# Sums of weights and low parts of weights by accumulating DMAs in the seven-product feed-forwards of a two-layer decoder

## The chip, the cores and the metric

One core of a Trainium2 chip. Its engines are TensorE (PE, matrix products), VectorE (DVE), ScalarE (ACT), GpSimd (POOL) and SyncE (SP, which here issues DMAs), beside 16 DMA engines that move data between HBM and SBUF and within SBUF. The metric is the device time of one execution in microseconds, lower is better; outputs are fp32.

## The reference

A decoder trunk of two layers on x of 512 tokens by 1024 channels; each layer is a half-step feed-forward, a mixer of three parallel groups, a cross-attention, and a second half-step feed-forward, with an RMSNorm ahead of each and one at the end. The change touches the feed-forwards:

```python
def swiglu_ffn(h, w_gate, w_up, w_down):
    return (jax.nn.silu(h @ w_gate) * (h @ w_up)) @ w_down
...
        h = rmsnorm(x, ffn1_norm[l])
        x = x + 0.5 * swiglu_ffn(h, ffn1_w_gate[l], ffn1_w_up[l], ffn1_w_down[l])
...
        h = rmsnorm(x, ffn2_norm[l])
        x = x + 0.5 * swiglu_ffn(h, ffn2_w_gate[l], ffn2_w_up[l], ffn2_w_down[l])
```

D_MODEL is 1024, D_FF is 2816.

## The kernel before

The phases run in the order ffn1, mixer, attention, ffn2 for layer 0, then the same for layer 1, then the final norm. An instruction's tile names carry phase and layer: ffn20 is ffn2 of layer 0, ffn11 is ffn1 of layer 1.

Every fp32 product is three products of a faster type: each operand is split into a hi part, rounded by a copy on ACT, and a lo part, what remains, by a subtraction on DVE. `mm3` issues hi weight by hi activation (L307), hi by lo (L308) and lo by hi (L309) or, where weights are the moving side, the same three.

The first feed-forward, ffn1 of layer 0, is a plain one (`ffn`). The other three go through `ffn7`, which works out gate and up products by a seven-product scheme: tokens are cut in two halves, the contraction in two halves kh, and gate and up (z = 0 and 1) are the two column halves, so a unit's weights are four quarters (kh, z) = (0,0), (1,0), (0,1), (1,1). A unit is four column blocks of 128 out of 22, so there are six units in an `ffn7`, the last of two blocks. Each unit makes products 1, 2, 5, 6, 3, 7, 4 in that order, with weights and activations that are sums or differences of quarters; the down products of the unit before stand between them. The weights that a product reads are:

- products 1 and 2: (0,0) and (1,0) as loaded
- product 5: t1 = gate rows plus up rows of the upper half, four tiles of 128x512 (`mix1`, L475 to L478, on DVE)
- product 6: (0,0) after (0,1) += (1,1) and (0,0) += (0,1); product 7 reads that (0,1) (`mix2`, L484 to L486, by `sum_`, L480 to L482, on DVE, two additions of 128x1024 for a sum)
- product 4: (1,0) after (1,0) += (0,0) (`mix3`)

The sums are made in place, in the raw quarters. Three rules set the order. `steps` holds products and down products; weights are split two steps ahead of their product (`split2`: one row of 128x1024, L448 and L450, and two rows of 128x512, L458 and L459, for a quarter), raw loads and sums are put in `before` at given steps, and the Tile scheduler, which orders each engine's queue by a simulated timeline, moves single instructions from there. An engine works its queue in order: where an instruction waits, all behind it on that engine waits.

The first unit of each `ffn7` is special. Its norm is a `PairNorm`: while the phase before ends, its `take` loads the four quarters of unit 0 ("wr_first_ffn"), and POOL makes t1 (L221) and (0,1) += (1,1) (L223); unit 0's other two sums are `sum_` at the next steps. As the residual x of each of the four 128-token tiles is finished (`add_x`, L372), `half` makes the mean square on ACT (L188), adds the two columns up on DVE (L190), raises to the power -1/2 on POOL (L191), and `emit` scales the tile on DVE (L234) and forms the differences that products 5 and 6 need (L239, L246, L248, L250). `give` transposes each on PE (L256) and splits it into hi on ACT (L258) and lo on DVE (L259). The splits of unit 0's weights for products 5 and on are issued after the last of these for product 5 (`marks`). The names that the steps use: xp and xc are transposed activations, the number behind the phase being tile and product; wh and wl are a weight's hi and lo ("wl_ffn20_0p10": unit 0, product 1, first row); px, py and pz are the accumulators of the products.

```python
G.tensor_tensor(out=ss[:, 3:4], in0=ss[:, 2:3], in1=nhalf[:, 0:1], op=ALU.pow)
...
if 2 <= i + 2 < 7:
    for z in norm.marks:
        es.enter_context(tc.issue_after(z))
w[i + 2] = steps[i + 2][1]()
```

Of the kernel before, what the change touches and what calls it, by code (L numbers as in the profile page):

```python
# [17 lines left out]
P = 128  # L18
# [26 lines left out]
def trunk_kernel(ctx: ExitStack, tc: tile.TileContext, io, out, phases=None):  # L45
    nc = tc.nc
    V, A, G, T = nc.vector, nc.scalar, nc.gpsimd, nc.tensor
    ADD, SUB, MUL = ALU.add, ALU.subtract, ALU.mult
# [41 lines left out]
    def vt(name, shape=(P, 512), dt=F32):  # L90
        return vp.tile(list(shape), dt, tag="V", name=name)
# [4 lines left out]
    def st(name, shape=(P, 512), dt=F32):  # L96
        return ssp.tile(list(shape), dt, tag="S", name=name)
# [36 lines left out]
    def tsl(t):  # L134
        return slice(t * P, (t + 1) * P)
# [68 lines left out]
    HK = NK // 2  # L204
# [227 lines left out]
    def ffn7(which, l, norm, nxt):  # L432


        wg, wu, wd = (io[f"{which}_w_{n}"][l] for n in ("gate", "up", "down"))
        units = [(f, min(4, NF - f)) for f in range(0, NF, 4)]
        hts, kept = {}, []
        steps, before, later = [], {}, []
        at_step = {}

        def split2(raws, name):

            got = []
            for s, raw in enumerate(raws):
                whole = s == 0 and len(raws) == 2
                if whole:
                    h = wp.tile(list(raw.shape), F32R, tag="wh", name=f"wh_{name}{s}")
                    A.activation(out=h, in_=raw, func=AF.Copy)  # L448
                    lo = wp.tile(list(raw.shape), F32R, tag="wl", name=f"wl_{name}{s}")
                    V.tensor_tensor(out=lo, in0=raw, in1=h.bitcast(F32), op=SUB)  # L450
                    got += [(h[:, k, :], lo[:, k, :]) for k in range(2)]
                    continue
                for k, r in enumerate([raw] if len(raws) == 4 else [raw[:, k, :] for k in range(2)]):
                    if len(raws) == 4 and s < 2:
                        h, lo = (wp.tile(list(r.shape), F32R, tag=f"w{z}", name=f"w{z}_{name}{s}") for z in "hl")
                    else:
                        h, lo = (st(f"w{z}_{name}{s}{k}", tuple(r.shape), F32R) for z in "hl")
                    A.activation(out=h, in_=r, func=AF.Copy)  # L458
                    V.tensor_tensor(out=lo, in0=r, in1=h.bitcast(F32), op=SUB)  # L459
                    got.append((h, lo))  # L460
            return got

        class Unit:
# [10 lines left out]
            def mix1(self):  # L474
                a, b = self.raw[0, 0], self.raw[0, 1]  # L475
                t1 = self.raw["t1"] = [vt(f"wt_{self.nm}{k}", (P, self.W)) for k in range(HK)]
                for k in range(HK):
                    V.tensor_tensor(out=t1[k], in0=a[k // 2][:, k % 2, :], in1=b[k // 2][:, k % 2, :], op=ADD)  # L478

            def sum_(self, to, other):  # L480
                for a, b in zip(self.raw[to], self.raw[other]):
                    V.tensor_tensor(out=a, in0=b, in1=a, op=ADD)  # L482

            def mix2(self):  # L484
                self.sum_((0, 1), (1, 1))
# [77 lines left out]
        for u, un in enumerate(us):  # L563
            b = len(steps)
# [812 lines left out]
```

## Time and profile before

| | |
|---|---|
| median of 3 runs | 2134.53 us (2134.12 to 2137.26) |
| profiled execution | 2135.13 us |
| its span | 2133.0 us |
| mean granted clock of PE | 0.987 |
| PE busy | 2065.5 us (97%) |
| DVE busy | 1551.3 us (73%) |
| ACT busy | 917.0 us (43%) |
| POOL busy | 356.8 us (17%) |
| DMA | 229.92 MB, mean 108 GB/s |

The profiled execution is the one that the trace shows, and its durations add up to its own time. Span is first to last instruction; what lies between it and the execution's time is before and after. A busy share is an average over the span. PEclk, the granted clock, is 1.00 at full speed.

### The profile page before, as it was taken

The numbers are of one execution on the slowest core, as the hardware profiler recorded it, in microseconds if no ns is written. First come the engines' busy times: TensorE is split into PE (matmuls) and PEld (weight loads), VectorE is DVE, ScalarE is ACT, GpSimd is POOL, SyncE is SP. The second block draws the span as 40 slices with busy tenths as digits, with TensorE's granted clock in tenths as the row PEclk, the third lists the DMA queues.
The fourth block names the chain that finished last, engine by engine and source line by source line (L and its number), as shares of the span: only waits on it lengthen the run. The fifth ranks groups of instructions, "written<-read, shape, count | busy, mean of one in ns | idle before, by whom it ended". The sixth has DMA issues, their size and how long they took to land.

```text
span 2133.0 us, 27561 instructions
## 1 busy us (share of the span) xinstructions
PE 2065.5 (97%) x10228; PEld 1732.9 (81%) x10228; DVE 1551.3 (73%) x2574; ACT 917.0 (43%) x1528; POOL 356.8 (17%) x349
## 2 busy tenths in 40 slices
PE   7999999999999999999999999999999999999998
PEld 6778788888788878888878888888877887888886
DVE  5755677579855788787688877666996458887765
ACT  4423333334534464454445444444344345554443
POOL 0377000155400200000110000013661020000000
PEclk9999999998999999999999999999999999999999
DMA  5332445343421323332314223263443232332222
GB/s 170 101 104 82 117 150 165 108 137 107 125 88 60 119 80 119 119 119 79 119 40 147 83 88 108 80 217 97 122 134 109 70 134 79 119 107 91 74 60 84
DMA packets 226750, 229.92 MB, mean 108 GB/s; under 512 B 38478, under 2 KB 152888, under 8 KB 226616
## 3 DMA queue, kind: packets, MB, share of 16 engines
q1 hardware_dynamic: 225952, 227.10, 34.3%
q8 instruction: 80, 1.31, 0.3%
q10 hardware_dynamic: 664, 1.07, 0.1%
q14 instruction: 54, 0.44, 0.1%
HBM read 213.77 MB, written 12.58 MB: 106 GB/s over the span
## 4 chain that ended last, share of the span: by engine, by line
PE 83%; DVE 8%; DMA 3%; ACT 3%; issue 2%; POOL 1%; SPq 1%; DVEq 0%; POOLq 0%; ACTq 0%
PE pxffn L308 6%; PE pxffn L309 6%; PE pxffn L307 6%; PE pddffn L308 5%; PE pddffn L309 5%; PE pddffn L307 5%; PE pzffn L307 3%; PE pzffn L308 3%; PE pzffn L309 3%; PE pdffn L309 2%; PE pdffn L307 2%; PE pdffn L308 2%; DVE cacc L1053 1%; PE qps L308 1%; PE qps L309 1%
## 5 line engine op out<-in xcount | busy, mean ns | idle before, releaser
L308 PE MATMUL pddffn<-wl_dffn,hhffn 128*128 128x512 f32 x480 | 188.9, 394 | 0.0
L309 PE MATMUL pddffn<-wh_dffn,hlffn 128*128 128x512 f32 x480 | 188.1, 392 | 0.0
L307 PE MATMUL pddffn<-wh_dffn,hhffn 128*128 128x512 f32 x480 | 185.8, 391 | 0.0
L1053 DVE SCALAR_TENSOR_TENSOR cacc<-ch,convw,cacc 128x510 f32<-128x510 f32 (+28 forms) x174 | 127.8, 735 | 6.2 <-ACT cacc L1051 2.5
L374 DVE SCALAR_TENSOR_TENSOR x<-pddffn,x 128x512 f32<-128x512 f32 x120 | 82.2, 686 | 62.8 <-PE pddffn L309 62.8
L308 PEld LDWEIGHTS pddffn<-wl_dffn,hhffn 128*128 128x128 f32 x480 | 90.2, 188 | 18.2
L309 PEld LDWEIGHTS pddffn<-wh_dffn,hlffn 128*128 128x128 f32 x480 | 90.2, 188 | 18.0
L307 PEld LDWEIGHTS pddffn<-wh_dffn,hhffn 128*128 128x128 f32 x480 | 89.8, 188 | 18.3
L221 POOL TENSOR_TENSOR wt_first_ffn<-wr_first_ffn,wr_first_ffn 128x512 f32<-128x512 f32 x12 | 16.8, 1426 | 503.3 <-DMA wr_first_ffn<-in_ffn_w_up_dram 503.3
L482 DVE TENSOR_TENSOR wr_ffn<-wr_ffn,wr_ffn 128x1024 f32<-128x1024 f32 (+1 forms) x90 | 98.4, 1110 | 0.1
L300 POOL TENSOR_TENSOR wl_pl<-wr_pl,wh_pl 128x1024 fp32r<-128x1024 f32 x4 | 9.6, 2404 | 486.0 <-ACT wh_pl L298 486.0
L459 DVE TENSOR_TENSOR wl_dffn<-wr_dffn,wh_dffn 128x512 fp32r<-128x512 f32 x60 | 42.0, 705 | 39.7 <-PE pxffn L308 18.2
L535 ACT ACTIVATE hhffn<-htffn 128x512 fp32r<-128x512 f32 x60 | 35.6, 594 | 80.7 <-PE htffn L529 80.6
L307 PE MATMUL pgffn<-xh_ffn,wh_gffn 128*128 128x512 f32 x168 | 66.2, 394 | 0.0
L308 PE MATMUL pgffn<-xl_ffn,wh_gffn 128*128 128x512 f32 x168 | 66.0, 393 | 0.0
L309 PE MATMUL pgffn<-xh_ffn,wl_gffn 128*128 128x512 f32 x168 | 65.9, 392 | 0.0
L309 PE MATMUL puffn<-xh_ffn,wl_uffn 128*128 128x512 f32 x168 | 65.8, 392 | 0.0
L307 PE MATMUL puffn<-xh_ffn,wh_uffn 128*128 128x512 f32 x168 | 65.8, 392 | 0.0
L308 PE MATMUL puffn<-xl_ffn,wh_uffn 128*128 128x512 f32 x168 | 65.8, 392 | 0.0
L191 POOL TENSOR_TENSOR ss_final<-ss_final,nhalf 128x1 f32<-128x1 f32 x4 | 2.2, 550 | 350.2 <-DVE ss_final L190 350.2
L307 PE MATMUL pdffn<-wh_dffn,h_ffffn 128*128 128x512 f32 x144 | 57.9, 402 | 2.1 <-DVE sffn L394 2.1
L300 POOL TENSOR_TENSOR wl_v<-wr_v,wh_v 128x1024 fp32r<-128x1024 f32 x22 | 53.5, 2441 | 35.4 <-ACT wh_v L298 25.7
(745 smaller groups left out, 6735.7 us busy)
## 6 DMA issues: line engine op xcount, KB each, us to landing
wr_dffn<-in_ffn_w_down_dram SPq DMA_DIRECT2D x78, 512.0 KB
wr_ffn<-in_ffn_w_up_dram SPq DMA_DIRECT2D x48, 512.0 KB
wr_ffn<-in_ffn_w_gate_dram SPq DMA_DIRECT2D x48, 512.0 KB
wr_gffn<-in_ffn_w_gate_dram SPq DMA_DIRECT2D x21, 512.0 KB
wr_uffn<-in_ffn_w_up_dram SPq DMA_DIRECT2D x21, 512.0 KB
wr_k<-in_xattn_wk_dram SPq DMA_DIRECT2D x16, 512.0 KB
wr_v<-in_xattn_wv_dram SPq DMA_DIRECT2D x16, 512.0 KB
wr_q<-in_xattn_wq_dram SPq DMA_DIRECT2D x16, 512.0 KB
```

The costliest lines, as they stand in the source:

```text
L191: G.tensor_tensor(out=ss[:, 3:4], in0=ss[:, 2:3], in1=nhalf[:, 0:1], op=ALU.pow)
L221: G.tensor_tensor(out=t1[k], in0=a[k // 2][:, k % 2, :], in1=b[k // 2][:, k % 2, :], op=ADD)
L300: (eng or V).tensor_tensor(out=lo, in0=raw, in1=h.bitcast(F32), op=SUB)
L307: T.matmul(ps, lhsT=wh, rhs=ah, start=first, stop=False, skip_group_check=skip)
L308: T.matmul(ps, lhsT=wh, rhs=al, start=False, stop=False, skip_group_check=skip)
L309: T.matmul(ps, lhsT=wl, rhs=ah, start=False, stop=last, skip_group_check=skip)
L374: V.scalar_tensor_tensor(out=x_, in0=ps, scalar=scale, in1=x_, op0=MUL, op1=ADD)
L459: V.tensor_tensor(out=lo, in0=r, in1=h.bitcast(F32), op=SUB)
L482: V.tensor_tensor(out=a, in0=b, in1=a, op=ADD)
L535: A.activation(out=h, in_=pt, func=AF.Copy)
L1053: V.scalar_tensor_tensor(out=acc[:, d:], in0=h[:, 0:S - d], scalar=cw[:, TAPS - 1 - d:TAPS - d], in1=acc[:, d:], op0=MUL, op1=ADD)
```

## The change

Three kinds of DVE work in `ffn7` become DMAs. An accumulating DMA (`accum_op=ADD`) adds what it moves to what stands in its destination; POOL issues all of these.

1. `mix1`: t1 of units 1 to 5 is no longer added up from the raw quarters. SP loads the gate rows from HBM into t1, and POOL issues DMAs that add the up rows from HBM to it. That is 60 loads and 60 accumulating DMAs, of 256 KB each in full units and 128 KB in the last.
2. `sum_`: every sum of quarters is an accumulating DMA from SBUF to SBUF, 90 in all, of 512 KB each in full units, those of unit 0 among them.
3. `low`: in unit 0 the lo parts of products 1 and 2 are made by a negated copy on ACT (raw weight into lo) and an accumulating DMA that adds the raw weight to it. The negated copy rounds to the type of lo just as the hi copy does, so what remains in lo is the raw weight less its hi part. That is six copies and six DMAs (512 KB for a row of 128x1024, 256 KB for one of 128x512) in each of the three `ffn7`.

DVE's queue is 180 rows shorter (2501 to 2321), POOL's 180 longer (343 to 523), ACT's 18 longer (1416 to 1434), SP's 60 longer.

```diff
--- before.py
+++ after.py
@@ -434,11 +434,19 @@
 
         wg, wu, wd = (io[f"{which}_w_{n}"][l] for n in ("gate", "up", "down"))
         units = [(f, min(4, NF - f)) for f in range(0, NF, 4)]
+        by_dma = (1, 2)
         hts, kept = {}, []
         steps, before, later = [], {}, []
         at_step = {}
 
-        def split2(raws, name):
+        def low(lo, raw, h, adding):
+            if adding:
+                A.activation(out=lo, in_=raw, func=AF.Copy, scale=-1.0)
+                G.dma_start(out=lo, in_=raw, accum_op=ADD)
+            else:
+                V.tensor_tensor(out=lo, in0=raw, in1=h.bitcast(F32), op=SUB)
+
+        def split2(raws, name, adding=False):
 
             got = []
             for s, raw in enumerate(raws):
@@ -447,7 +455,7 @@
                     h = wp.tile(list(raw.shape), F32R, tag="wh", name=f"wh_{name}{s}")
                     A.activation(out=h, in_=raw, func=AF.Copy)
                     lo = wp.tile(list(raw.shape), F32R, tag="wl", name=f"wl_{name}{s}")
-                    V.tensor_tensor(out=lo, in0=raw, in1=h.bitcast(F32), op=SUB)
+                    low(lo, raw, h, adding)
                     got += [(h[:, k, :], lo[:, k, :]) for k in range(2)]
                     continue
                 for k, r in enumerate([raw] if len(raws) == 4 else [raw[:, k, :] for k in range(2)]):
@@ -456,7 +464,7 @@
                     else:
                         h, lo = (st(f"w{z}_{name}{s}{k}", tuple(r.shape), F32R) for z in "hl")
                     A.activation(out=h, in_=r, func=AF.Copy)
-                    V.tensor_tensor(out=lo, in0=r, in1=h.bitcast(F32), op=SUB)
+                    low(lo, r, h, adding)
                     got.append((h, lo))
             return got
 
@@ -475,11 +483,15 @@
                 a, b = self.raw[0, 0], self.raw[0, 1]
                 t1 = self.raw["t1"] = [vt(f"wt_{self.nm}{k}", (P, self.W)) for k in range(HK)]
                 for k in range(HK):
-                    V.tensor_tensor(out=t1[k], in0=a[k // 2][:, k % 2, :], in1=b[k // 2][:, k % 2, :], op=ADD)
+                    r0 = k * P
+                    nc.sync.dma_start(out=t1[k], in_=wg[r0:r0 + P, self.f0 * P:self.f0 * P + self.W])
+                for k in range(HK):
+                    r0 = k * P
+                    G.dma_start(out=t1[k], in_=wu[r0:r0 + P, self.f0 * P:self.f0 * P + self.W], accum_op=ADD)
 
             def sum_(self, to, other):
                 for a, b in zip(self.raw[to], self.raw[other]):
-                    V.tensor_tensor(out=a, in0=b, in1=a, op=ADD)
+                    G.dma_start(out=a, in_=b, accum_op=ADD)
 
             def mix2(self):
                 self.sum_((0, 1), (1, 1))
@@ -501,7 +513,7 @@
                                 k == HK - 1, True)
                     for t in range(2):
                         post(t)
-                steps.append((run, lambda: split2(self.raw[src], f"{self.nm}p{i}")))
+                steps.append((run, lambda: split2(self.raw[src], f"{self.nm}p{i}", self.u == 0 and i in by_dma)))
 
             def keep(self, c, name):
                 def post(t):
```

Line numbers below L437 move; `low` is L442 to L447 in the changed kernel, with the negated copy on L444 and its DMA on L445, the hi copy of a whole row on L456, t1's load and DMA on L487 and L490 and the sum's DMA on L494.

POOL's queue at the start of ffn2 of layer 0, before: (0,1) += (1,1) by two additions, then the powers of the four token tiles (ss_ffn20*t*).

```order
L221 TENSOR_TENSOR wt_first_ffn202_6379<-wr_first_ffn20001_6363,wr_first_ffn20011_6371 128x512
L221 TENSOR_TENSOR wt_first_ffn203_6380<-wr_first_ffn20001_6363,wr_first_ffn20011_6371 128x512
L223 TENSOR_TENSOR wr_first_ffn20010_6369<-wr_first_ffn20110_6373,wr_first_ffn20010_6369 128x1024
L223 TENSOR_TENSOR wr_first_ffn20011_6371<-wr_first_ffn20111_6375,wr_first_ffn20011_6371 128x1024
L191 TENSOR_TENSOR ss_ffn200_6404<-ss_ffn200_6404,nhalf_99 128x1
L191 TENSOR_TENSOR ss_ffn201_6443<-ss_ffn201_6443,nhalf_99 128x1
L191 TENSOR_TENSOR ss_ffn202_6501<-ss_ffn202_6501,nhalf_99 128x1
L191 TENSOR_TENSOR ss_ffn203_6554<-ss_ffn203_6554,nhalf_99 128x1
```

The same place in the changed kernel; wr_first_ffn20*kz s* is quarter (k,z), row s.

```order
L223 TENSOR_TENSOR wr_first_ffn20010_6369<-wr_first_ffn20110_6373,wr_first_ffn20010_6369 128x1024
L223 TENSOR_TENSOR wr_first_ffn20011_6371<-wr_first_ffn20111_6375,wr_first_ffn20011_6371 128x1024
L191 TENSOR_TENSOR ss_ffn200_6404<-ss_ffn200_6404,nhalf_99 128x1
L494 DMA wr_first_ffn20001_6363<-wr_first_ffn20011_6371 128x1024
L191 TENSOR_TENSOR ss_ffn201_6443<-ss_ffn201_6443,nhalf_99 128x1
L445 DMA wl_ffn20_0p211_6626<-wr_first_ffn20101_6367 128x512
L191 TENSOR_TENSOR ss_ffn202_6501<-ss_ffn202_6501,nhalf_99 128x1
L494 DMA wr_first_ffn20101_6367<-wr_first_ffn20001_6363 128x1024
L445 DMA wl_ffn20_0p10_6602<-wr_first_ffn20000_6361 128x1024
L445 DMA wl_ffn20_0p20_6617<-wr_first_ffn20100_6365 128x1024
L494 DMA wr_first_ffn20000_6361<-wr_first_ffn20010_6369 128x1024
L191 TENSOR_TENSOR ss_ffn203_6554<-ss_ffn203_6554,nhalf_99 128x1
```

The powers of the last three tiles now stand between DMAs; the low of product 1's first row (0p10) stands behind the sum into (1,0) row 1, and the last power behind the sum into (0,0) row 0, which overwrites what the DMA of 0p10 reads.

PE's queue where product 1 of unit 0 of the same phase begins, before: pxffn20_0*t* is its accumulator for token tile t of each half.

```order
L256 MATMUL xp_ffn2011_6478<-ident_90,xn_ffn2010_6476 128x128 x4
L307 MATMUL pxffn20_00_6640<-wh_ffn20_0p10_6600,xc_ffn201_6387 128x512
L256 MATMUL xp_ffn2012_6487<-ident_90,xn_ffn2011_6485 128x128 x4
L308 MATMUL pxffn20_00_6640<-wl_ffn20_0p10_6602,xc_ffn201_6387 128x512
L309 MATMUL pxffn20_00_6640<-wh_ffn20_0p10_6600,xc_ffn201_6387 128x512
L307 MATMUL pxffn20_00_6640<-wh_ffn20_0p10_6600,xc_ffn201_6387 128x512
L308 MATMUL pxffn20_00_6640<-wl_ffn20_0p10_6602,xc_ffn201_6387 128x512
L309 MATMUL pxffn20_00_6640<-wh_ffn20_0p10_6600,xc_ffn201_6387 128x512
```

And in the changed kernel:

```order
L256 MATMUL xp_ffn2011_6478<-ident_90,xn_ffn2010_6476 128x128 x4
L307 MATMUL pxffn20_00_6646<-wh_ffn20_0p10_6600,xc_ffn201_6387 128x512
L256 MATMUL xp_ffn2012_6487<-ident_90,xn_ffn2011_6485 128x128 x4
L307 MATMUL pxffn20_01_6647<-wh_ffn20_0p10_6600,xc_ffn201_6387 128x512
L307 MATMUL pyffn20_00_6706<-wh_ffn20_0p20_6615,xc_ffn202_6388 128x512
L308 MATMUL pxffn20_00_6646<-wl_ffn20_0p10_6602,xc_ffn201_6387 128x512
L309 MATMUL pxffn20_00_6646<-wh_ffn20_0p10_6600,xc_ffn201_6387 128x512
L308 MATMUL pxffn20_01_6647<-wl_ffn20_0p10_6602,xc_ffn201_6387 128x512
L307 MATMUL pxffn20_00_6646<-wh_ffn20_0p10_6600,xc_ffn201_6387 128x512
L308 MATMUL pxffn20_00_6646<-wl_ffn20_0p10_6602,xc_ffn201_6387 128x512
```

A first hi product for the second token tile and one of product 2 (pyffn20) moved ahead of the first product that reads the low wl_ffn20_0p10.

DVE's queue between the column sums (L190) of the third and the last token tile of that norm, before:

```order
L234 SCALAR_TENSOR_TENSOR xn_ffn2020_6534<-x2_103,ss_ffn202_6501,gb_ffn200_6357 128x512
L234 SCALAR_TENSOR_TENSOR xn_ffn2021_6536<-x2_103,ss_ffn202_6501,gb_ffn201_6358 128x512
L450 TENSOR_TENSOR wl_ffn20_0p10_6602<-wr_first_ffn20000_6361,wh_ffn20_0p10_6600 128x1024
L450 TENSOR_TENSOR wl_ffn20_0p20_6614<-wr_first_ffn20100_6365,wh_ffn20_0p20_6612 128x1024
L239 TENSOR_TENSOR xs_ffn202_6538<-xn_ffn2021_6536,xn_ffn2020_6534 128x512
L372 TENSOR_TENSOR x3_104<-pwo0_31_6557,x3_104 128x512
L482 TENSOR_TENSOR wr_first_ffn20000_6361<-wr_first_ffn20010_6369,wr_first_ffn20000_6361 128x1024
L259 TENSOR_TENSOR xc_ffn201_6387<-xp_ffn2011_6478,xc_ffn201_6387 128x4x128
L259 TENSOR_TENSOR xc_ffn202_6388<-xp_ffn2012_6487,xc_ffn202_6388 128x4x128
L250 TENSOR_TENSOR xn_ffn2020_6534<-xn_ffn2000_6418,xn_ffn2020_6534 128x512
L190 TENSOR_SCALAR ss_ffn203_6554<-ss_ffn203_6554 128x1
L482 TENSOR_TENSOR wr_first_ffn20100_6365<-wr_first_ffn20000_6361,wr_first_ffn20100_6365 128x1024
```

And in the changed kernel:

```order
L190 TENSOR_SCALAR ss_ffn202_6501<-ss_ffn202_6501 128x1
L259 TENSOR_TENSOR xc_ffn201_6387<-xp_ffn2001_6420,xc_ffn201_6387 128x4x128
L234 SCALAR_TENSOR_TENSOR xn_ffn2020_6534<-x2_103,ss_ffn202_6501,gb_ffn200_6357 128x512
L234 SCALAR_TENSOR_TENSOR xn_ffn2021_6536<-x2_103,ss_ffn202_6501,gb_ffn201_6358 128x512
L259 TENSOR_TENSOR xc_ffn202_6388<-xp_ffn2002_6429,xc_ffn202_6388 128x4x128
L239 TENSOR_TENSOR xs_ffn202_6538<-xn_ffn2021_6536,xn_ffn2020_6534 128x512
L250 TENSOR_TENSOR xn_ffn2020_6534<-xn_ffn2000_6418,xn_ffn2020_6534 128x512
L372 TENSOR_TENSOR x3_104<-pwo0_31_6557,x3_104 128x512
L259 TENSOR_TENSOR xc_ffn201_6387<-xp_ffn2011_6478,xc_ffn201_6387 128x4x128
L190 TENSOR_SCALAR ss_ffn203_6554<-ss_ffn203_6554 128x1
L259 TENSOR_TENSOR xc_ffn202_6388<-xp_ffn2012_6487,xc_ffn202_6388 128x4x128
L234 SCALAR_TENSOR_TENSOR xn_ffn2030_6587<-x3_104,ss_ffn203_6554,gb_ffn200_6357 128x512
```

The two lows of products 1 and 2 (L450) and the sums into (0,0) and (1,0) (L482) no longer stand on DVE between the tile's parts.

## Rows read from the trace of the kernel before

**Rows 1.** The page's busy times, share of the span and instructions of each engine.

```profile
PE 2065.5 (97%) x10228; PEld 1732.9 (81%) x10228; DVE 1551.3 (73%) x2574; ACT 917.0 (43%) x1528; POOL 356.8 (17%) x349
```

**Rows 2.** Busy times by stretch, in later units; the columns stand in the first line.

```profile
core 0: us, PE busy (x) PEld busy (x) DVE busy (x) ACT busy (x) POOL busy (x), PEclk, DMA share, GB/s
800.00:900.00 100.00, 100.00 (x455) 82.69 (x454) 81.40 (x111) 44.90 (x67) 0.00 (x0) 1.00 0.41 127
```

**Rows 3.** The same view at the first units of ffn20, ffn11 (two) and ffn21.

```profile
745.00:760.00 15.00, 12.06 (x55) 9.35 (x54) 14.32 (x24) 10.49 (x18) 0.00 (x0) 0.89 0.06 11
1100.00:1120.00 20.00, 16.77 (x76) 13.23 (x75) 17.38 (x27) 11.90 (x20) 0.00 (x0) 0.91 0.11 28
1120.00:1130.00 10.00, 9.17 (x40) 7.25 (x40) 6.15 (x8) 5.51 (x9) 0.00 (x0) 1.00 0.95 334
1775.00:1795.00 20.00, 16.88 (x77) 13.38 (x77) 18.62 (x29) 11.99 (x21) 1.25 (x1) 0.91 0.10 26
```

**Rows 4.** Timeline of PE: start, duration, line, tiles; in brackets idle before it, releaser.

```profile
736.67 0.49 PE L308 MATMUL pxffn<-wl_ffn_0p,xc_ffn 128*128 128x512 f32 x1
...
747.97 1.03 PE L256 MATMUL xp_ffn<-ident,xs_ffn 128*128 128x128 f32 x8
750.27 0.63 PE L256 MATMUL xp_ffn<-ident,xs_ffn 128*128 128x128 f32 x4 [1.27 <-DVE xc_ffn L259]
752.24 0.68 PE L307 MATMUL pxffn<-wh_ffn_0p,xc_ffn 128*128 128x512 f32 x1 [1.34 <-ACT xc_ffn L258]
```

**Rows 5.** Timeline of DVE in the same stretch.

```profile
734.62 2.35 DVE L450 TENSOR_TENSOR wl_ffn_0p<-wr_first_ffn,wh_ffn_0p 128x1024 fp32r<-128x1024 f32 x2
...
738.10 1.21 DVE L482 TENSOR_TENSOR wr_first_ffn<-wr_first_ffn,wr_first_ffn 128x1024 f32<-128x1024 f32 x1
...
741.03 0.20 DVE L190 TENSOR_SCALAR ss_ffn<-ss_ffn 128x1 f32<-128x1 f32 x1
...
742.81 1.41 DVE L234 SCALAR_TENSOR_TENSOR xn_ffn<-x,ss_ffn,gb_ffn 128x512 f32<-128x512 f32 x2 [0.45 <-POOL ss_ffn L191]
```

**Rows 6.** Timeline of POOL at the first units of ffn20 and ffn11.

```profile
741.31 1.46 POOL L191 TENSOR_TENSOR ss_ffn<-ss_ffn,nhalf 128x1 f32<-128x1 f32 x1 [8.49 <-DVE ss_ffn L190]
...
1063.32 2.40 POOL L223 TENSOR_TENSOR wr_first_ffn<-wr_first_ffn,wr_first_ffn 128x1024 f32<-128x1024 f32 x1 [0.74 <-DMA wr_first_ffn<-in_ffn_w_up_dram]
1071.18 5.58 POOL L223 TENSOR_TENSOR wr_first_ffn<-wr_first_ffn,wr_first_ffn 128x1024 f32<-128x1024 f32 x1 [5.46 <-DMA wr_first_ffn<-in_ffn_w_up_dram]
1088.53 0.55 POOL L191 TENSOR_TENSOR ss_ffn<-ss_ffn,nhalf 128x1 f32<-128x1 f32 x1 [11.77 <-DVE ss_ffn L190]
```

**Rows 7.** Groups by line on DVE, whole kernel: count, busy us, mean ns, idle before.

```profile
L482 DVE TENSOR_TENSOR wr_ffn<-wr_ffn,wr_ffn 128x1024 f32<-128x1024 f32 (+1 forms) x90 | 98.4, 1110 | 0.1
L478 DVE TENSOR_TENSOR wt_ffn<-wr_ffn,wr_ffn 128x512 f32<-128x512 f32 (+1 forms) x60 | 36.0, 634 | 9.4 <-DMA wr_ffn<-in_ffn_w_up_dram 9.3
```

**Rows 8.** Timelines of DVE, ACT and PE in unit 2 of ffn20.

```profile
845.84 1.22 DVE L482 TENSOR_TENSOR wr_ffn<-wr_ffn,wr_ffn 128x1024 f32<-128x1024 f32 x1
...
857.29 1.06 ACT L448 ACTIVATE wh_ffn_2p<-wr_ffn 128x1024 fp32r<-128x1024 f32 x1 [1.61 <-PE pyffn L309]
...
865.75 0.39 PE L307 MATMUL pxffn<-wh_ffn_2p,xc_ffn 128*128 128x512 f32 x1
```

**Rows 9.** Timeline of ACT at the first unit of ffn20.

```profile
728.83 0.63 ACT L458 ACTIVATE wh_ffn_0p<-wr_first_ffn 128x512 fp32r<-128x512 f32 x1 [5.06 <-PE pwo L309]
...
732.21 2.00 ACT L448 ACTIVATE wh_ffn_0p<-wr_first_ffn 128x1024 fp32r<-128x1024 f32 x2
```

**Rows 10.** Transfers in the chain of waits: start, duration, destination, source (512 KB; sdy 256 KB).

```profile
1530.06 3.40 DMA sdy<-ssw
1537.28 3.66 DMA wr_k<-in_xattn_wk_dram
...
1737.60 5.66 DMA wr_first_ffn<-in_ffn_w_gate_dram
```

**Rows 11.** Timelines of ACT and PE where unit 1 of ffn20 begins.

```profile
776.39 1.05 ACT L448 ACTIVATE wh_ffn_1p<-wr_ffn 128x1024 fp32r<-128x1024 f32 x1
...
781.17 0.62 PE L307 MATMUL pxffn<-wh_ffn_1p,xc_ffn 128*128 128x512 f32 x2
```

## The prediction

> **What bounds the kernel now.** I began with the busy times: TensorE (PE) is busy 97% of the span and VectorE (DVE) 73% [rows 1]. Such shares are averages, so next came the busy times by stretch: from 800 to 900 us, in the later units of a seven-product feed-forward, PE is busy in every microsecond at full clock, and DVE 81% [rows 2]. DVE time that is taken away there buys nothing. PE has something to give only where it idles, and I found one such stretch in each of the three seven-product feed-forwards, at the start of product 6 of the first unit [rows 3]. From 745 to 760 us PE is busy 12.06 of 15, so 2.94 us idle, at a mean granted clock of 0.89: on the busy part, 11% of 12.06 is 1.3 us. From 1100 to 1120 it is 3.23 us idle at 0.91, from 1775 to 1795 3.12 us at 0.91. All three together hold 9.3 us of idle time and about 4 us of clock: 13 us is all that there is to win.
>
> Last came what PE waits for at 750 us, followed back by the timelines. Product 6 starts at 752.24 after a hi-half copy of ACT, and the transposes ahead of it, 750.27, after DVE [rows 4]. DVE has run almost without a gap since 742.81, where it waited for POOL's power at 741.31 [rows 5, 6]. That power came late because DVE made the column sum for it (L190) only at 741.03, behind a sum of weights at 738.10 and two lows of weights, 2.35 us, at 734.62 [rows 5]. So DVE is the bound of this stretch, and what stands on it there is just what the change takes off.
>
> **The change part by part.**
>
> *t1 and the sums of the later units.* The change takes 90 sums, 98.4 us, and 60 t1 additions, 36.0 us, off DVE [rows 7]. In the later units PE covers all of it [rows 2]: no gain. Their price could only be lateness. In unit 2 the sums into (0,0) began at 845.84 and product 6, their first reader on PE, at 865.75; the last hi copy for it ran at 857.29 for 1.06 us [rows 8]. If copies and lows keep some 9 of these 20 us, a landing may take about 11 us before PE sees it. If that cover is gone, each of 15 later units pays the rest. I take nothing.
>
> *Lows of products 1 and 2.* For each of three first units six subtractions leave DVE: two of 128x1024 (2.35 us together [rows 5]) and four of 128x512, about 0.7 each, so 5.2 us, and four sums of 1.2 us. ACT takes on six negated copies, two of 1.00 and four of 0.63 by its own hi copies [rows 9]: 4.5 us. POOL issues ten accumulating DMAs.
>
> *What replaces them on the critical stretch.* No row shows an accumulating DMA, nor any that POOL issues. The nearest rows: 512 KB from HBM took 3.66 and 5.66 us, 256 KB from SBUF 3.40 [rows 10]. An accumulating DMA reads its destination too, so for 512 KB (t512) I take the slow end, 5.7, and for 256 KB (t256) 3.4, which can't well be below it by more. The ends I keep for t512 are 3.7, and twice the slowest, 11.3, every destination byte being moved twice. Anything below 3.7 gains nothing more, as there is no wait left to end.
>
> The Trainium skill's page "DMA: Bandwidth & Descriptors", section "Anatomy of one DMA — SWDGE (gpsimd) path", fits 2.0 us plus the bytes at 436 GB/s to a DMA that GpSimd issues: an estimate of 3.2 us for 512 KB, which no run here shows. By it the sum would be that of rival 1.
>
> The chain in ffn2_0: ACT's copy for product 2's last quarter row ran at 728.83 for 0.63 us [rows 9]; the negated copy stands beside it, so its DMA leaves POOL at about 730.1. POOL's next sum, into (1,0), overwrites what that DMA reads and waits for its landing, 733.5. Behind it stands the DMA of product 1's first low (wl 0p10), whose negated copy is done at about 733.3; it lands at 733.5 + 5.7 = 739.2. PE read that low at 736.67 [rows 4]; two hi matmuls of 0.22 us (455 in 100 us [rows 2]) now go first, so PE wants it at 737.1. Stall: 2.1 us. On the same queue the last power (L191) stands behind a sum that waits for the same landing: it runs at about 739.8, where it ended at 742.77 before (741.31 + 1.46 [rows 6]). DVE, relieved, is ready for it, so product 6's chain comes over 2 us earlier than 752.24. PE would be through product 2 and the transposes at 747.97 + 1.03 = 749.0 [rows 4], say 749.3 to its next matmul; with the stall product 6 starts at 751.4: 0.8 us earlier than before. Of the 1.3 us of clock none or all comes back, as PE still idles 2.1 us, only sooner: 0.8 to 2.1, middle 1.4. ffn2_1 has the same order and the same gap: again 1.4.
>
> *ffn1_1.* Here the lows of products 1 and 2 are made some 20 us before they are read, and all of POOL's DMAs for them stand ahead of its first power at 1088.53 [rows 6]. The last DVE rows before the gap are unchanged. I count nothing; the bounds are the 3.2 us idle there as a gain and rival 3 as a loss.
>
> Sum: 2 x 1.4 = 2.8 off 2135.13, the profiled execution, is 2132.3. That execution stands 0.6 above the median of 2134.53, so against the runs I forecast **2132** (2131.7 rounded). A measurement of this kernel can tell about 0.2%, 4.3 us, from no change: the forecast is no change that it can tell, with a small gain in it.
>
> **The rivals.** Product 6 starts at 749.3 + (730.1 + t256 + t512 - 737.1) = 742.3 + t256 + t512, as long as that is later than 749.3. The two DMA times decide, and 9.9 us together is where gain turns to loss.
>
> 1. *Quick DMAs.* With 3.4 and 3.7 product 6 starts at 749.4, 2.8 earlier, and 1.3 of clock comes back: 4.1 twice, 8.2, so 2126.9, and 2126.3 against the median. For it: the quickest row [rows 10], and DMA engines all but idle there, share 0.06 [rows 3]. Against: the second read, and that three DMAs stand one behind another.
>
> 2. *Slow accumulating DMAs*, the case on the other side: one queue, POOL's, holds both product 1's low and the last power, and from 9.9 us on for the pair the change loses. At 5 and 8 us product 6 starts at 755.3, 3.1 late, twice 6.2: 2141.3. At 6.8 and 11.3 it is 8.2 late, twice 16.4: 2151.5. For it: nothing in the trace bounds the read and write of a destination. Against: plain 512 KB stay under 6 us [rows 10].
>
> 3. *POOL held up beside DVE.* The same addition, L223, took 2.40 us at 1063.32 and 5.58 at 1071.18 [rows 6]: 3.2 us more with only its neighbours changed. If issuing a DMA suffers alike, two such waits lie in the chain, 6.4 us: start 757.8, 5.6 late, twice 11.2, 2146.3. The Trainium skill's page "SBUF — State Buffer", section "SBUF: two separate sides", has a rule that speaks against the change: a DMA issued from GpSimd waits for its descriptors while DVE runs in its two-port mode. By that rule rival 3 would hold; the two rows of L223 show POOL waiting beside others, and no run here shows a DMA doing so.
>
> 4. *The new traffic.* The second units start in a stretch where the DMA engines are busy 95% at 334 GB/s [rows 3]. On SP's queue unit 1's four t1 loads now stand ahead of its quarters (0,0), (1,0) and half of (0,1) and (1,1), and POOL adds four more transfers of 256 KB: 2.1 MB, 6.3 us at that rate. Weights for unit 1 are first copied at 776.39 and multiplied at 781.17 [rows 11]. If all 6.3 us reached PE less the 4.8 between these two, 1.5 us in three places, 4.5 in all, 2139.6; with destination reads as well, 9.4 us, it is 13.8: 2148.9. Against: DMA engines are idle before, so that half of it may pass early.
>
> 5. *Nothing reaches PE.* What bounds product 6 turns out to be other than DVE's queue: 2135, told from the forecast only by the gap.
>
> **How the numbers follow.** My forecast with rival 5, no change that can be told: 0.42. Rival 1: 0.30. Rival 2: 0.15, rival 3: 0.06, rival 4 with lateness in later units: 0.07, together 0.28 for slower. The range runs from rival 1, 2126, to rival 3, 2146; outside it lie the slow ends of rivals 2 and 4 and a gain in ffn1_1 on top of rival 1. The likeliest case's own range is 2130 to 2135.
>
> **What would show it.** Right: in ffn2_0 and ffn2_1 product 1 waits about 2 us for a DMA at its first low, the gap before product 6 shrinks to under 1 us, ffn1_1's gap stays, and in later units PE stays at 100% with DVE some 12% lower. Quick side: no such wait and the clock at 1.00 after 750. Slow side: a wait of 6 us or more there with the last power late, or PE waiting for DMA in later units, which would break the 11 us of cover.

## The result, and the profile after

Median 2147.34 us (4 runs, 2146.60 to 2149.44) against 2134.36: a ratio of 1.0056, 95% interval 1.0041 to 1.0071. The changed kernel is slower by 13 us, just above the top of the range. The profiled execution took 2149.44, with a span of 2147.7.

The page's busy times of the changed kernel:

```profile
PE 2071.5 (96%) x10228; PEld 1735.7 (81%) x10228; DVE 1409.9 (66%) x2394; ACT 932.2 (43%) x1546; POOL 508.1 (24%) x529
```

Its DMA issues by POOL: destination and source, count, KB each, median us from issue to landing:

```profile
wr_ffn<-wr_ffn POOLq DMA_DIRECT2D x72, 512.0 KB, 4.9
wr_first_ffn<-wr_first_ffn POOLq DMA_DIRECT2D x12, 512.0 KB, 4.5
wl_ffn_0p<-wr_first_ffn POOLq DMA_DIRECT2D x12, 256.0 KB, 7.2
wl_ffn_0p<-wr_first_ffn POOLq DMA_DIRECT2D x6, 512.0 KB, 6.4
```

DVE lost 141 us against [rows 1], and PE's end did not come sooner by any of it. Busy times by stretch, with the columns of [rows 2], in the first unit of ffn20 and in later units:

```profile
730.00:740.00 10.00, 6.45 (x31) 4.90 (x30) 6.11 (x10) 6.47 (x12) 3.34 (x5) 0.98 0.81 157
740.00:750.00 10.00, 10.00 (x44) 8.14 (x43) 4.90 (x8) 1.99 (x4) 2.06 (x3) 0.85 0.66 131
750.00:760.00 10.00, 8.51 (x35) 6.16 (x34) 10.00 (x17) 7.48 (x14) 2.66 (x3) 0.83 0.53 130
...
800.00:900.00 100.00, 100.00 (x455) 82.71 (x454) 64.84 (x91) 46.06 (x69) 13.17 (x16) 1.00 0.75 198
```

In later units PE stays at 100%, with DVE at 65% instead of 81% and the DMA engines at 0.75 instead of 0.41 [rows 2]: t1 and the sums there cost nothing and bring nothing. In the first unit the same stretches of the kernel before were:

```profile
730.00:740.00 10.00, 10.00 (x54) 8.39 (x53) 9.96 (x15) 6.73 (x14) 0.55 (x1) 1.00 0.01 2
740.00:750.00 10.00, 9.00 (x46) 7.33 (x44) 9.14 (x15) 3.08 (x6) 1.46 (x1) 1.00 0.00 1
750.00:760.00 10.00, 8.06 (x33) 6.16 (x34) 9.74 (x17) 8.50 (x15) 0.00 (x0) 0.83 0.08 16
```

PE now idles 3.55 of the ten us from 730 on, where it was busy throughout, and a second stretch, 740 to 750, has a lowered clock (0.85, where it was 1.00): behind its wait PE starts matmuls 0.43 us apart from 739.87 to 742.86, and 0.23 apart after. These are the lower and the upper of its two levels, 1.2 and 2.4 GHz. PE's waits there, and those like them in ffn11 (1095.01) and ffn21 (1785.56), from the timeline of PE:

```profile
709.64 0.50 PE L307 MATMUL pwo<-wh_xo,h_o 128*128 128x512 f32 x1 [1.39 <-ACT h_o L314]
...
739.38 0.70 PE L308 MATMUL pxffn<-wl_ffn_0p,xc_ffn 128*128 128x512 f32 x1 [3.21 <-DMA wl_ffn_0p<-wr_first_ffn]
...
753.34 0.50 PE L307 MATMUL pxffn<-wh_ffn_0p,xc_ffn 128*128 128x512 f32 x1
754.34 0.49 PE L307 MATMUL pxffn<-wh_ffn_0p,xc_ffn 128*128 128x512 f32 x1 [0.50 <-ACT xc_ffn L258]
...
1095.01 1.32 PE L256 MATMUL xp_ffn<-ident,xn_ffn 128*128 128x128 f32 x8 [1.70 <-DVE xn_ffn L234]
...
1785.56 0.79 PE L308 MATMUL pxffn<-wl_ffn_0p,xc_ffn 128*128 128x512 f32 x1 [3.37 <-DMA wl_ffn_0p<-wr_first_ffn]
```

PE now waits 3.21 and 3.37 us for product 1's low, and in ffn11 1.70 us for DVE, which waits for POOL. The timelines of POOL and, last, of DVE say why (a DMA's duration here is its issue alone):

```profile
728.52 0.89 POOL L445 DMA_DIRECT2D wl_ffn_0p<-wr_first_ffn  x1 [4.22 <-ACT wl_ffn_0p L444]
...
732.35 0.88 POOL L494 DMA_DIRECT2D wr_first_ffn<-wr_first_ffn  x1 [1.92 <-DMA wl_ffn_0p<-wr_first_ffn]
732.93 1.18 POOL L445 DMA_DIRECT2D wl_ffn_0p<-wr_first_ffn  x1
...
739.73 0.87 POOL L494 DMA_DIRECT2D wr_first_ffn<-wr_first_ffn  x1 [4.49 <-DMA wl_ffn_0p<-wr_first_ffn]
740.29 0.89 POOL L191 TENSOR_TENSOR ss_ffn<-ss_ffn,nhalf 128x1 f32<-128x1 f32 x1
...
1083.96 0.89 POOL L445 DMA_DIRECT2D wl_ffn_0p<-wr_first_ffn  x1 [2.46 <-ACT hhlffn L547]
...
1092.72 0.86 POOL L494 DMA_DIRECT2D wr_first_ffn<-wr_first_ffn  x1 [4.34 <-DMA wl_ffn_0p<-wr_first_ffn]
1093.29 0.88 POOL L191 TENSOR_TENSOR ss_ffn<-ss_ffn,nhalf 128x1 f32<-128x1 f32 x1
...
1094.20 1.41 DVE L234 SCALAR_TENSOR_TENSOR xn_ffn<-x,ss_ffn,gb_ffn 128x512 f32<-128x512 f32 x2 [2.76 <-POOL ss_ffn L191]
```

The sum at 732.35 overwrites what the DMA issued at 728.52 reads, so it waited for that landing, and product 1's low stood behind it. The sum at 739.73 overwrites what that low's DMA reads: it waited 4.49 us, with the last power (L191) behind it. In ffn11 the same wait, 4.34 us, holds a power at 1093.29, and PE waits for what DVE makes with it. The transfers themselves stand in the chain of waits (start, duration, what moved):

```profile
728.52 3.19 DMA wl_ffn_0p<-wr_first_ffn
732.93 6.40 DMA wl_ffn_0p<-wr_first_ffn
```

The two add up to 9.59 us.

To place the loss I measured, on PE, from the first product with the last phase's kept rows (before: 677.20, 1078.73, 1710.86) to the first product of unit 2. The table gives that stretch, less its length before (171.23, 127.75, 171.88 us), in each profiled execution, and the timed ratio to the kernel before on the same chip; the other kernels are those of the next section. Single runs of one kernel spread by several us on the chip of the experiments, so verdicts go by the ratio's interval, and places by the stretches.

| kernel | ffn20 | ffn11 | ffn21 | sum, us | ratio (95%) |
|---|---|---|---|---|---|
| changed | +5.5 | +1.7 | +4.2 | +11.4 | 1.0056 (1.0041 to 1.0071) |
| lows_dve | +0.5 | -1.8 | +1.4 | 0.0 | 0.9990 (0.9976 to 1.0005) |
| lows_only | +2.7 | +6.3 | +4.5 | +13.6 | 1.0049 (1.0035 to 1.0063) |
| later_only | +0.3 | +0.2 | +1.3 | +1.8 | 1.0001 (0.9987 to 1.0015) |
| p2_dma | +3.2 | -2.5 | +4.8 | +5.5 | 1.0038 (1.0024 to 1.0051) |
| after_pow_first | +2.4 | +0.8 | +2.4 | +5.6 | 1.0023 (1.0011 to 1.0036) |
| pow_first | +0.4 | -1.8 | +1.4 | -0.1 | 0.9991 (0.9978 to 1.0004) |
| low_pool_add | +3.3 | -0.3 | +2.8 | +5.8 | 1.0028 (1.0015 to 1.0040) |
| copy_only | +2.3 | +0.9 | +1.8 | +5.0 | 1.0005 (0.9993 to 1.0016) |
| mark3 | +0.5 | +3.1 | +2.4 | +6.0 | 1.0016 (1.0002 to 1.0031) |
| nomark | +3.6 | +2.9 | +3.4 | +9.9 | 1.0055 (1.0036 to 1.0073) |
| before_mark3 | +0.3 | -2.3 | -0.8 | -2.7 | 0.9972 (0.9958 to 0.9986) |
| pow_first_mark3 | -0.2 | -4.1 | -1.7 | -6.0 | 0.9968 (0.9957 to 0.9979) |

Between the two profiled executions the span grew by 14.7 us (2133.0 to 2147.7), and 11.4 of these lie in the three stretches. Each row is one execution against one: later_only leaves every operation of a first unit on its engine, and still differs by 1.3 us in ffn21; copy_only's sum of 5.0 is above the 3.4 us that its ratio allows; and p2_dma's execution, 2139.60, is its quickest, with a median of 2145.94. A difference of about a microsecond is therefore not read.

### The profile page after: what moved, and what is told of

Same layout as the page of the kernel before. It is cut to its first block, busy times and chain, and to the rows that moved or that the text cites. A ratio compares the mean times of both kernels' runs of the same rounds, so it can differ in the third digit from the quotient of the medians.

```text
span 2147.7 us, 28130 instructions
## 1 busy us (share of the span) xinstructions
PE 2071.5 (96%) x10228; PEld 1735.7 (81%) x10228; DVE 1409.9 (66%) x2394; ACT 932.2 (43%) x1546; POOL 508.1 (24%) x529
## 4 chain that ended last, share of the span: by engine, by line
PE 80%; DVE 8%; DMA 5%; ACT 3%; issue 2%; POOL 2%; SPq 1%; DVEq 0%; POOLq 0%; ACTq 0%
PE pxffn L308 6%; PE pxffn L309 5%; PE pxffn L307 5%; PE pddffn L308 5%; PE pddffn L309 5%; PE pddffn L307 5%; PE pzffn L307 2%; PE pzffn L308 2%; PE pzffn L309 2%; PE pdffn L309 2%; PE pdffn L307 2%; DMA wl_ffn_0p<-wr_first_ffn 1%; PE pdffn L308 1%; PE qps L308 1%; PE qps L309 1%
## 5 line engine op out<-in xcount | busy, mean ns | idle before, releaser
L494 POOL DMA_DIRECT2D wr_ffn<-wr_ffn x90 | 78.3, 884 | 578.5 <-DVE x L374 183.7
L308 PE MATMUL pddffn<-wl_dffn,hhffn 128*128 128x512 f32 x480 | 189.0, 394 | 0.0
L447 DVE TENSOR_TENSOR wl_dffn<-wr_dffn,wh_dffn 128x512 fp32r<-128x512 f32 (+1 forms) x90 | 75.0, 865 | 67.7 <-ACT wh_dffn L456 26.2
L308 PEld LDWEIGHTS pddffn<-wl_dffn,hhffn 128*128 128x128 f32 x480 | 90.2, 188 | 18.3
L490 POOL DMA_DIRECT2D wt_ffn<-in_ffn_w_up_dram x60 | 53.1, 1010 | 155.9 <-DMA wt_ffn<-in_ffn_w_gate_dram 91.5
L308 PE MATMUL pgffn<-xl_ffn,wh_gffn 128*128 128x512 f32 x168 | 66.0, 393 | 0.0
L308 PE MATMUL puffn<-xl_ffn,wh_uffn 128*128 128x512 f32 x168 | 65.8, 392 | 0.0
L445 POOL DMA_DIRECT2D wl_ffn_0p<-wr_first_ffn x18 | 16.7, 947 | 199.0 <-PE pv_31a L309 186.6
L548 DVE TENSOR_TENSOR hlffn<-htffn,hhffn 128x512 fp32r<-128x512 f32 x60 | 41.2, 686 | 30.3 <-ACT hhffn L547 30.3
L308 PE MATMUL qps<-xl_att,wh_q 128*128 128x256 f32 (+1 forms) x176 | 60.0, 341 | 0.0
```

Of the source, the lines that this page charges most:

```text
L445: G.dma_start(out=lo, in_=raw, accum_op=ADD)
L490: G.dma_start(out=t1[k], in_=wu[r0:r0 + P, self.f0 * P:self.f0 * P + self.W], accum_op=ADD)
L494: G.dma_start(out=a, in_=b, accum_op=ADD)
L548: V.tensor_tensor(out=lo, in0=pt, in1=h.bitcast(F32), op=SUB)
```

## The experiments

Three theories were held against each other. The times in the first four expectations count from a kernel before at about 2134; the chip of those experiments ran it at 2137.27, so they are compared by the ratio. A: the lows by DMA stand on the critical path of the first units, by their landings and by what queues behind them. B: the loss comes from the traffic and late weights of the later units. C: unit 0's sums, now on POOL's queue, hold the powers of the norm.

**lows_dve**, the changed kernel with

```diff
-        by_dma = (1, 2)
+        by_dma = ()
```

> The changed kernel with the lows of products 1 and 2 back on DVE (no negated copies, no DMAs for lows); t1 and all sums stay DMAs. Theory A (PE waits for the 512 KB low of product 1, and the powers stand behind the landings of lows on POOL's queue): the 3.2 and 3.4 us waits for wl_ffn_0p are gone, ffn11's 1.7 us wait too, 2133 to 2137. Theory B (the new DMA traffic and t1 in later units): stays at 2145 to 2147. Theory C (the sums of unit 0 on POOL's queue hold the last power): 2140 to 2145, with the last power of ffn20 still as late as 740.

The ratio fell to 0.9990: all of the loss is gone, as A says, and what is left of the change is worth nothing that can be told. By the table ffn11 is 1.8 us shorter than before, here and in pow_first, and ffn21 1.4 longer; neither was followed. C was half right. Timelines of POOL, DVE and PE:

```profile
739.25 0.88 POOL L494 DMA_DIRECT2D wr_first_ffn<-wr_first_ffn  x1 [4.15 <-issue]
739.81 0.90 POOL L191 TENSOR_TENSOR ss_ffn<-ss_ffn,nhalf 128x1 f32<-128x1 f32 x1
...
740.74 1.42 DVE L234 SCALAR_TENSOR_TENSOR xn_ffn<-x,ss_ffn,gb_ffn 128x512 f32<-128x512 f32 x2 [2.56 <-POOL ss_ffn L191]
...
749.93 0.50 PE L307 MATMUL pxffn<-wh_ffn_0p,xc_ffn 128*128 128x512 f32 x1 [0.79 <-ACT xc_ffn L258]
```

The sums do hold the power, 2.56 us of DVE's time, and nothing is slower for it.

**lows_only**: `sum_` and `mix1` as before, `low` as in the change.

> The kernel before with only the lows of products 1 and 2 of first units by DMA; t1 and all sums on DVE. Theory A: most of the loss is here, 2142 to 2148, with a wait of 3 us or more of PE for wl_ffn_0p in ffn20 and ffn21. Theory B: 2133 to 2136. Theory C: 2136 to 2140 (the DMAs for lows stand on POOL's queue, the sums don't).

1.0049: A. PE's wait for the low is shorter here than the 3 us that A asked for, and a new one appears (timelines of PE and DVE):

```profile
731.66 0.51 PE L308 MATMUL pxffn<-wl_ffn_0p,xc_ffn 128*128 128x512 f32 x1 [1.06 <-DMA wl_ffn_0p<-wr_first_ffn]
...
1085.14 1.23 DVE L490 TENSOR_TENSOR wr_first_ffn<-wr_first_ffn,wr_first_ffn 128x1024 f32<-128x1024 f32 x1 [4.77 <-issue]
...
1087.12 0.47 PE L307 MATMUL plffn<-wh_lastffn,hhlffn 128*128 128x512 f32 x1 [4.55 <-DVE x L374]
```

The low's 512 KB took 4.4 us here (median of the list), 6.4 in the changed kernel, where a sum is in flight beside it. In ffn11 DVE's sum, which overwrites what a low's DMA reads, stood 4.77 us on DVE's queue (the profile names no releaser; that low was issued at 1075.03 and took 10.0 us to landing), and the residual behind it made PE wait 4.55: a wait for a DMA's reading moved to whichever queue makes the sum.

**later_only**: lows and unit 0's sums on DVE.

```diff
-        by_dma = (1, 2)
+        by_dma = ()
...
+                    if self.u == 0:
+                        V.tensor_tensor(out=a, in0=b, in1=a, op=ADD)
+                    else:
                         G.dma_start(out=a, in_=b, accum_op=ADD)
```

> The kernel before with only t1 and the sums of units 1 to 5 by DMA; unit 0 as before. Theory A and C: 2132 to 2136, no different from before, although 120 of 134 us of DVE work and all of the t1 traffic have moved. Theory B: 2142 to 2147.

1.0001: theory B falls. All of t1 and 78 of 90 sums, 116 us of DVE's busy time (1551.3 to 1435.2), can be moved for nothing.

**p2_dma**: `by_dma = (2,)` and no more.

> The changed kernel with the lows of product 1 on DVE and only those of product 2 by DMA. Theory A: the wait for product 1's low goes, a wait for product 2's takes its place, as it is needed 2 to 4 us later: 2137 to 2143. Theory B: 2145 to 2147. Theory C: 2143 to 2147, as all sums stay on POOL.

1.0038, 2142.5 on a kernel before of 2134.4: inside A's range, but the interval (2139.5 to 2145.2) reaches into C's, so that by its time this run does not part the two; lows_dve does. The wait moved to product 2's low, at L308 of pyffn, 1.64 us in ffn20 and 3.34 in ffn21. ffn11, where the lows are early, lost nothing.

**after_pow_first**: all DMAs of the change, their order on POOL changed.

```diff
+                self.pw = G.tensor_tensor(out=ss[:, 3:4], in0=ss[:, 2:3], in1=nhalf[:, 0:1], op=ALU.pow).ins
...
+                    with tc.issue_after(norm.pw) if self.u == 0 else nullcontext():
+                        G.dma_start(out=a, in_=b, accum_op=ADD)
```

> The changed kernel, all DMAs kept, but unit 0's four sums are issued on POOL only after the last power (L191). If the loss is in the order on POOL's queue (the low of product 1 stands behind a sum that waits for the landing of another low, and the powers behind sums that wait for lows): ffn11's wait of 1.7 us for L234 goes, the low's DMA is issued up to 2 us sooner and, with one accumulating DMA fewer beside it, takes 4.4 as in lows_only and not 6.4, PE's wait for it falls from 3.2 to 1 us: 2135 to 2139 where before is 2134, a ratio of 1.001 to 1.003. If the loss is in the lows by DMA whatever the queue: 1.004 to 1.006.

1.0023: the order on POOL's queue is part of the loss, more than half of it by the middle values (the intervals, 1.0011 to 1.0036 and 1.0041 to 1.0071, do not meet but are wide). Timeline of PE:

```profile
737.38 0.50 PE L308 MATMUL pxffn<-wl_ffn_0p,xc_ffn 128*128 128x512 f32 x1 [1.16 <-DMA wl_ffn_0p<-wr_first_ffn]
```

1.16 instead of 3.21; the low took 4.7 in the list instead of 6.4, and ffn11's wait for L234 is gone.

**pow_first**: the same order with lows on DVE (`by_dma = ()`).

> Lows on DVE, t1 and sums by DMA, unit 0's sums after the last power. In lows_dve the last power of ffn20 ran at 739.81 although its column sum was done at 738.19, held by a sum that waited for a landing; here it runs at 738.3, product 6 starts 1 to 1.6 us sooner in ffn20 and ffn21: ratio to before 0.997 to 0.999. If something else bounds product 6: the same as lows_dve, 0.999.

A miss, and the most useful one. Timelines of DVE, ACT and PE:

```profile
740.62 1.41 DVE L234 SCALAR_TENSOR_TENSOR xn_ffn<-x,ss_ffn,gb_ffn 128x512 f32<-128x512 f32 x2 [0.66 <-POOL ss_ffn L191]
...
748.55 1.66 ACT L466 ACTIVATE wh_ffn_0p<-wt_first_ffn 128x512 fp32r<-128x512 f32 x3
...
751.70 0.49 PE L307 MATMUL pxffn<-wh_ffn_0p,xc_ffn 128*128 128x512 f32 x1 [0.79 <-ACT xc_ffn L258]
```

Product 1 began at 736.63 here and at 734.86 in lows_dve. Counted from it, L234 runs at 3.99 us instead of 5.88, and product 6 starts at 15.07 in both: 1.9 us on the norm's chain reach nothing. PE's own order has the last transposes behind product 2, and ACT's splits, held by the mark behind product 5's copies, come next.

**low_pool_add**: POOL adds the raw weights up, no DMA for lows.

```diff
-                G.dma_start(out=lo, in_=raw, accum_op=ADD)
+                G.tensor_tensor(out=lo, in0=lo.bitcast(F32), in1=raw, op=ADD)
```

> The changed kernel with each low's accumulating DMA replaced by an addition on POOL at the same place of its queue (2.4 us for 128x1024 by L223 alone, up to 5.6 beside DVE); the negated copies on ACT stay. Theory that the DMA's landing (6.4 us and the waits behind it) is the cost: no wait for DMA before product 1's first low, ffn20 and ffn21 lose under 2 us each and not 4 to 5.5, ratio 1.000 to 1.003. Theory that ACT's negated copies or the reordering of PE is the cost: 1.004 to 1.006 as in the changed kernel.

1.0028, within the first theory's range: no wait for a low at product 1, and by the middle values half of the loss gone. But 3 us a stretch remain in ffn20 and ffn21, more than expected; POOL spent 5.64 us on the two whole lows at 730.82, and PE waited 1.88 us for h_o. What of the rest is POOL's, what ACT's copies and what PE's new order was not separated.

**copy_only**: the kernel before with the 18 negated copies, which DVE's subtractions overwrite.

```diff
+            if adding:
+                A.activation(out=lo, in_=raw, func=AF.Copy, scale=-1.0)
...
```

> The kernel before, with nothing added but the 18 negated copies on ACT, whose results DVE's subtractions write over. It shows what ACT's share of the changed kernel costs by itself: in the changed kernel and in low_pool_add PE waited 1.4 to 1.9 us for ACT's hi copy of the attention's output ahead of ffn20 and of ffn21 (0.2 before). If that is ACT's copies standing ahead of it: 1.2 us in ffn20 and in ffn21 each, ratio 1.001 to 1.002. If the copies cost nothing by themselves: 0.999 to 1.001, and that wait stays at 0.2.

1.0005: not told apart from nothing. PE's wait for h_o in its profile is 0.75 us ahead of ffn20 and 1.58 ahead of ffn21, so the copies do stand ahead of the attention's output; the timed cost is at most 0.16%.

**mark3** loosens the rule that pow_first pointed at, in lows_dve; **before_mark3** does the same in the kernel before, **nomark** drops the rule in lows_dve.

```diff
-                    if 2 <= i + 2 < 7:
+                    if 3 <= i + 2 < 7:
```

> As lows_dve (lows on DVE, t1 and sums by DMA), but product 5's weight splits are no longer held behind the last transposed copy for product 5 (marks only from product 6 on). In lows_dve ACT was idle 3.5 us before 741.9 and then made three splits of t1 and one of (0,0) between that mark and the copies that product 6 waits for. If ACT's order is what bounds product 6, product 6 starts 1 to 1.7 us sooner in each of three feed-forwards: ratio to lows_dve 0.998 to 0.999, to before 0.996 to 0.998. If DVE or PE's own order bounds it: as lows_dve, 0.999.

> The kernel before with only that rule loosened. If ACT's order alone is the bound, the gain is the same without any DMA: 0.997 to 0.999. If DVE's queue is the second bound behind it, less than in mark3 or nothing: 0.999 to 1.001.

> As mark3 with no hold at all on the splits of products 5, 6, 3, 7 and 4. ACT-bound: at least as good as mark3, 0.995 to 0.998. If early splits get in the way of the transposed copies on ACT or DVE: worse than mark3, 0.999 to 1.002.

before_mark3 gains (0.9972) without any DMA; mark3 loses (1.0016), a miss; nomark loses most (1.0055), more than I had put at worst. Early splits get in the way there: product 6 starts sooner in ffn20, 14.51 us after product 1, but PE then waits 2.74 us inside it for a low that DVE makes (L447, at 750.33), and unit 1 begins 48.6 us after product 1, where it was 45.2. Timelines of POOL and DVE in mark3:

```profile
738.51 0.88 POOL L494 DMA_DIRECT2D wr_first_ffn<-wr_first_ffn  x1 [5.23 <-DVE ss_ffn L190]
739.04 2.13 POOL L490 DMA_DIRECT2D wt_ffn<-in_ffn_w_up_dram  x2
740.38 1.38 POOL L191 TENSOR_TENSOR ss_ffn<-ss_ffn,nhalf 128x1 f32<-128x1 f32 x1
...
741.79 1.42 DVE L234 SCALAR_TENSOR_TENSOR xn_ffn<-x,ss_ffn,gb_ffn 128x512 f32<-128x512 f32 x2 [3.63 <-POOL ss_ffn L191]
```

The last power stands behind a sum and two t1 issues. The profile puts the sum's wait down to DVE's column sum, which ended at 738.16; but by the kernel's order this sum reads what the sum ahead of it on the queue (issued at 732.39, 5.5 us to landing) writes, and it was issued 0.6 us behind that landing, as in lows_dve (734.22, 4.4 us to landing, then 739.25). I take it that the landing was the wait. With the mark loosened this is the bound, and DVE waits 3.63 us.

**pow_first_mark3** takes that away: mark3 with unit 0's sums and unit 1's t1 additions issued after the last power.

> mark3 with unit 0's sums (and unit 1's t1 additions) issued on POOL after the last power. In mark3 the last power ran 3.6 us after DVE could use it, held by a sum that waited for a landing, in before_mark3 it did not. If that hold is what made mark3 slower than before_mark3: 0.995 to 0.998, at or below before_mark3's 0.9972. If the DMAs cost something else in the first units: 1.000 to 1.002 as mark3.

0.9968: the hold was it. This and before_mark3 beat the kernel before by about 0.3%; their intervals overlap, so the DMAs are not shown to be worth anything beyond the loosened mark. In before_mark3's profile 2.7 us of the gain lie in the three stretches, of about 6 by its ratio; the rest is not placed.

## Why the prediction was wrong

*What bounds the kernel, later units.* Right: PE at 100% [rows 2], and 116 us of DVE time given away for nothing (later_only).

*The stall.* The mechanism was right, its size low: PE waited 3.21 us where 2.1 were forecast. t256 was 3.19 (3.4 taken) and t512 6.40 (5.7 taken): 0.7 is a term of the sum that was mis-sized, an accumulating DMA with another beside it, 4.4 when it has none (lows_only). Some 1.2 were put at nothing: the low's DMA left POOL 1.25 us ahead of product 1's start (734.18 - 732.93) where 2.5 were taken (736.00 - 733.5), as POOL issued the sum 0.64 us behind the landing at 731.71 and the low 0.58 behind the sum. Against that PE wanted the low 0.9 us later than taken, behind three hi matmuls and a wait of 0.33. By the fit in the Trainium skill's page "DMA: Bandwidth & Descriptors", section "Anatomy of one DMA — SWDGE (gpsimd) path", 512 KB would take 3.2 us, an estimate. The trace does not agree: the low took 6.40 here and 4.4 alone.

*The gain against it: the step that failed.* I took it that "DVE is the bound of this stretch", so that product 6 would start at the end of product 2 plus the stall, without the gap of [rows 3]. Counted from product 1's start its first matmul came at 16.24 us before (752.24 - 736.00), at 19.16 in the changed kernel (753.34 - 734.18), 2.9 later where I had 0.8 sooner. In lows_dve and pow_first, with all sums off DVE and no stall, it is 15.07: relief is worth 1.2 us, not 2.9, and unit 1 of ffn20 begins 45.2 us after product 1 in before, lows_dve and pow_first alike (49.9 in the changed kernel). The trace had a hint: the row at 752.24 waits for ACT, not DVE [rows 4], and ACT's splits stood between the mark and that copy. Timeline of ACT, before:

```profile
748.60 0.60 ACT L258 ACTIVATE xc_ffn<-xp_ffn 128x512 fp32r<-128x512 f32 x1 [2.11 <-PE xp_ffn L256]
```

and in the changed kernel:

```profile
749.69 0.60 ACT L258 ACTIVATE xc_ffn<-xp_ffn 128x512 fp32r<-128x512 f32 x1 [2.33 <-PE xp_ffn L256]
750.19 1.66 ACT L466 ACTIVATE wh_ffn_0p<-wt_first_ffn 128x512 fp32r<-128x512 f32 x3
751.75 1.05 ACT L456 ACTIVATE wh_ffn_0p<-wr_first_ffn 128x1024 fp32r<-128x1024 f32 x1
752.70 0.58 ACT L258 ACTIVATE xc_ffn<-xp_ffn 128x512 fp32r<-128x512 f32 x1
```

The first of these copies is product 5's last; behind it ACT makes four splits and then the copy that product 6 reads. From that first copy to product 6 it is 3.64 us before (748.60 to 752.24) and 3.65 in the changed kernel (749.69 to 753.34), and so in lows_dve and pow_first: what leaves DVE does not shorten it, and it begins when PE makes product 5's last transposes, behind most of products 1 and 2. The two chains are in series, and I had taken the later of them. So the stall delayed those transposes and was paid, and of the gap's waits, 1.27, 1.34 and 0.32 us before, 0.50 stayed for ACT and 0.97 for a low that DVE makes.

*Clock.* I expected none or all of 1.3 us back; instead a second stretch fell to 0.85. Weighted by PE's busy time, 740 to 760 costs 1.5 + 1.4 us, where before 750 to 760 alone was at 0.83: about 1.5 more. With waits of 7.2 us (PE's waits over 0.2 us from 700 to 780) where there were 3.8, that is 4.9 of ffn20's 5.5.

*What was costed at nothing.* ACT's copies: "4.5 us" were listed, with no word on h_o, which stands behind two of them: PE waits 1.39 us for it (at 709.64 in the timeline above) where it waited 0.23 before. ffn1_1: I argued that all DMAs stand ahead of its first power and so are done; they stand ahead on the queue, and sums among them wait for landings. They took from 1068.34 to 1092.72, the power came at 1093.29, and it cost 1.7 us.

*The rivals.* Rival 1 did not happen: the pair of DMAs took 9.6 us and not 7.1. Rival 2 happened, by the pair t256 + t512 of 9.6 us, under the 9.9 that I had given as its point: the point was wrong, for the reason above. Rival 3 did not: POOL's DMA issues take 0.85 to 1.18 us each in the first units, beside a working DVE; the rule that I set beside this rival asks for DVE's two-port mode, and no row shows which mode DVE was in. Rival 4 did not (later_only). Rival 5 was right in what bounds product 6, ACT's order and not DVE's queue, but not in its time, as the stall was paid all the same.

3.3 of the 14.7 us lie outside the three stretches and are not placed; the mixers move by several us from one profiled execution to the next, in kernels that are no slower too.

## What to carry to other kernels

Before an engine is relieved, follow the gap to its end: an idle stretch whose last wait is for another engine need not shrink by the time taken off the busy one. A DMA that takes an operation's place brings its landing into every queue that later overwrites its source, and whatever stands behind that waits too, however small (here a power of 128 numbers). Where such DMAs must be, issue them behind the short operations that others wait for.

## What the hardware showed that was not expected

An accumulating DMA of 512 KB from SBUF to SBUF, issued by POOL, takes 4.4 us from issue to landing alone and 6.4 beside another (8.0 and 9.6 in p2_dma's chain, behind two sums in flight); one of 256 KB took 3.19 with none beside it (728.52), and 7.2 as the median of all lows of that size. The DMA engines are 81% busy where the lows run, and by accumulating DMAs alone. The queue that POOL issues to, from 730 to 740 (packets, MB, share of the 16 engines):

```profile
q0 software_dynamic: 494, 1.57, 81.2%
```

That is 157 GB/s at a share of 0.81, where the loads of [rows 3] moved 334 at 0.95: per byte counted the accumulating DMAs held the engines 1.8 times as long.

A few us of idle PE cost more than their length: in the ten us behind the wait of 3.2 the granted clock was 0.85, where it was 1.00 before.
